# A two-expert combine on one core: the weights fetched as 16 long rows and turned by TensorE, in place of 128 short rows

## The chip, the cores and the metric

The kernel runs on one core of one Trainium2 chip. The metric is device time in microseconds (us), the median over several runs. Inside the core the work is done by TensorE (PE), VectorE (DVE), ScalarE (ACT) and GpSimd (POOL); SyncE (SP) issues transfers. Transfers between device memory and the on-chip memory are carried by 16 DMA engines, which two queues feed here: one that SP issues to (q1 in the profile) and one that ACT issues to (q10).

## The reference

Each of 16 x 1024 = 16384 tokens has two vectors of 512 numbers, one from each of its two experts, and two weights. The result is the weighted sum of the two vectors, in float32:

```
expert_outputs   (16, 1024, 2, 512)   float32
combine_weights  (16, 1024, 2)        float32
out[b, s, :] = expert_outputs[b, s, 0, :] * combine_weights[b, s, 0]
             + expert_outputs[b, s, 1, :] * combine_weights[b, s, 1]
```

There are 67 MB to read, 33.5 MB to write, and 131 KB of weights.

## The kernel before

**Layout.** The 16384 tokens are spread over 128 partitions, 128 tokens to a partition. The first 115 x 128 tokens (LAST = 115) are dealt out as 115 consecutive tokens per partition, the remaining 13 x 128 as 13 per partition; `rows` (lines 41 to 45) makes the views of both parts. A token's slot on a partition is its two expert vectors, 4 KB. The large tile `et` (line 58) has 51 such slots, divided into four rooms of 13, 13, 12 and 13 slots (lines 29 to 31). The tile `wt` (line 60) holds the weights in the form in which they are used: partition p has the two weights of each of its 128 tokens.

**Loop.** The tokens are worked in ten groups of 12 or 13 slots (line 32). Group g lies in room g mod 4. For each group `combine` (line 79) multiplies the whole room by its weights with one VectorE instruction (line 98) and adds the two halves with another (line 99), in place; the result goes back to device memory with one store (line 121). Group 8 (lines 87 to 95) and group 9 (lines 83 to 86) share the multiplication with ScalarE. When a room's store has landed, the load of the group four further on may go into it (line 124). So the fifth load waits for the first store, and so on.

**Queues.** All loads are issued by SP, in the order of the groups. The first one is in two parts (lines 110 and 111): two slots, cut into pieces of 4 KB, and the other 11. Loads two to four (groups 1 to 3) follow at once, as their rooms are free. The stores of groups 0 to 6 are issued by ACT, those of groups 7 to 9 by SP (line 120). The schedule is manual: each engine runs its instructions in the order in which they stand in the code, and waits where the data that it reads, or the room that it writes, isn't free.

**The start.** Before the loop three small transfers go to ACT's queue. VectorE fills a tile `zt` of 16 partitions x 128 numbers with zeros (line 102); ACT writes it to 16 places of the output, which are overwritten later (line 105). Then ACT fetches the weights with two transfers (lines 106 and 107): 128 rows of 115 x 2 numbers (920 bytes), one to each partition, and 128 rows of 13 x 2 numbers (104 bytes). VectorE's first multiplication (line 98) needs the weights and group 0.

Of the kernel before, what the change touches and what calls it, by code (L numbers as in the profile page):

```python
# [1 line left out]

# [4 lines left out]


@with_exitstack
def kernel(  # L10
    ctx: ExitStack,
    tc: tile.TileContext,
    expert_outputs: bass.AP,
    combine_weights: bass.AP,
    out: bass.AP,
):

    nc = tc.nc
    b, s, k, h = expert_outputs.shape
    assert k == 2
    n = b * s
    P = nc.NUM_PARTITIONS
    per = n // P
    assert per * P == n

    SIZES = [13, 13, 12, 13]
    ROOMS = len(SIZES)  # L30
    ROOM0 = [sum(SIZES[:r]) for r in range(ROOMS)]
    TILES = [13, 13, 12, 13, 13, 13, 12, 13, 13, 13]
    FIRST = [2, 11, 13, 12, 13]
    STORES = [[0], [1], [2], [3], [4], [5], [6], [7], [8], [9]]
    MIXED = {8: 3}
    LAST = 115
    N = len(TILES)
    assert sum(TILES) == per
    starts = [sum(TILES[:g]) for g in range(N)]

    def rows(x):

        first = x[0 : P * LAST, :].rearrange("(p t) f -> p t f", p=P)
        second = x[P * LAST : n, :].rearrange("(p t) f -> p t f", p=P)
        return lambda t, c: first[:, t : t + c, :] if t < LAST else second[:, t - LAST : t - LAST + c, :]

    flat = out.rearrange("b s h -> (b s) h")
    eo = rows(expert_outputs.rearrange("b s k h -> (b s) (k h)"))
    cw = rows(combine_weights.rearrange("b s k -> (b s) k"))
    o = rows(flat)  # L50

    dt = mybir.dt.float32
    mult = mybir.AluOpType.mult
    add = mybir.AluOpType.add
    copy = mybir.ActivationFunctionType.Copy

    pool = ctx.enter_context(tc.tile_pool(name="all", bufs=1))
    et = pool.tile([P, sum(SIZES), k * h], dt)
    halves = et.rearrange("p j (k h) -> p (j k) h", k=k)
    wt = pool.tile([P, per * k], dt)  # L60
    wk = wt.rearrange("p (t k) -> p t k", k=k)
    zt = pool.tile([16, 128], dt)
    warm = pool.tile([P, 1], dt)

    def load(g, skip=0, c=None, **kw):
        c = TILES[g] - skip if c is None else c
        at = ROOM0[g % ROOMS] + skip
        nc.sync.dma_start(out=et[:, at : at + c], in_=eo(starts[g] + skip, c), **kw)  # L68

    def weights(q, t, c):  # L70
        q.dma_start(out=wk[:, t : t + c, :], in_=cw(t, c))

    def pair(t, x0, x1, y):
        nc.scalar.activation(out=x0, in_=x0, func=copy, scale=wt[:, k * t : k * t + 1])  # L74
        nc.vector.scalar_tensor_tensor(  # L75
            out=y, in0=x1, scalar=wt[:, k * t + 1 : k * t + 2], in1=x0, op0=mult, op1=add
        )

    def combine(g, base):
        at, c, t0 = ROOM0[g % ROOMS], TILES[g], starts[g]  # L80
        room = halves[:, k * at : k * (at + c), :]
        x0, x1 = et[:, at : at + c, 0:h], et[:, at : at + c, h : 2 * h]
        if g == N - 1:
            for i in range(c):
                pair(t0 + i, x0[:, i, :], x1[:, i, :], halves[:, base + i, :])
            return
        if g in MIXED:
            v = MIXED[g]
            for i in range(v, c):
                x = x0[:, i, :]  # L90
                nc.scalar.activation(out=x, in_=x, func=copy, scale=wt[:, k * (t0 + i) : k * (t0 + i) + 1])  # L91
            w0 = wk[:, t0 : t0 + v, 0:1].to_broadcast([P, v, h])
            nc.vector.tensor_tensor(out=x0[:, 0:v, :], in0=x0[:, 0:v, :], in1=w0, op=mult)  # L93
            w1 = wk[:, t0 : t0 + c, 1:2].to_broadcast([P, c, h])
            nc.vector.tensor_tensor(out=x1, in0=x1, in1=w1, op=mult)  # L95
        else:
            wb = wt[:, k * t0 : k * (t0 + c)].unsqueeze(2).to_broadcast([P, k * c, h])
            nc.vector.tensor_tensor(out=room, in0=room, in1=wb, op=mult)  # L98
        nc.vector.tensor_tensor(out=halves[:, base : base + c, :], in0=x0, in1=x1, op=add)  # L99

    with tc.manual_schedule():
        nc.vector.memset(zt, 0.0)  # L102

        ahead = flat[0 : P * LAST, :].rearrange("(q t) h -> q (t h)", q=16)
        nc.scalar.dma_start(out=ahead[:, 0:128], in_=zt)  # L105
        weights(nc.scalar, 0, LAST)
        weights(nc.scalar, LAST, per - LAST)
        nc.scalar.activation(out=warm, in_=nc.const_aps.tensor(1.0, (P, 1), dt), func=copy)  # L108

        load(0, 0, 2, max_dma_last_dim=k * h * 4)  # L110
        load(0, 2)
        for g in range(1, ROOMS):
            load(g)
        for j, st in enumerate(STORES):
            base = k * ROOM0[st[0] % ROOMS if st != [N - 1] else (N - 4) % ROOMS]
            c = 0
            for g in st:
                combine(g, base + c)
                c += TILES[g]
            q = nc.sync if j >= 7 else nc.scalar  # L120
            q.dma_start(out=o(starts[st[0]], c), in_=halves[:, base : base + c, :])
            for g in st:
                if g + ROOMS < N:
                    load(g + ROOMS)


# [1 line left out]
_INS = ['expert_outputs', 'combine_weights']  # L128
_OUTS = [((16, 1024, 512), 'float32')]


# [23 lines left out]
```

## Time and profile before

| | |
|---|---|
| median of 3 runs | 239.11 us (239.08 to 239.14) |
| the profiled execution | 238.84 us |
| its span, first to last instruction | 237.1 us |
| VectorE busy | 190.0 us |
| ScalarE busy | 15.8 us |
| read / written in device memory | 67.24 MB / 33.56 MB |

The span is what the profile shows in detail; some 1.7 us of the execution's time lie around it. "Busy" counts the time in which an engine runs an instruction, not the time in which it waits. A packet is one piece of a transfer that one DMA engine moves: here, as a rule, what goes to one partition in one row, and 16 closing packets of 4 bytes with each transfer. A share in a row of a DMA queue is the packets' time, as a part of 16 engines over the stretch that was asked for; in short stretches a packet counts where it starts, so a share can be over 100%.

### The profile page before, as it was taken

How to read it: one execution, taken by the hardware profiler on the slowest of the kernel's cores; microseconds unless marked ns; L12 is line 12 of the kernel's file. 1: busy time of each engine (PE TensorE's matmuls, PEld its weight loads, DVE VectorE, ACT ScalarE, POOL GpSimd, SP SyncE). 2: the span in 40 equal slices, each digit the busy share in tenths (PEclk: the TensorE clock that was granted, in tenths of full speed). 3: DMA queues.
4: the chain of work that ended last, by engine and by line, in shares of the span. 5: the costliest groups of instructions: out<-in, count | busy, mean ns of one | idle time of the engine just before them, and what ended most of it. 6: DMA issues, size and time to landing. Idle time of an engine off the chain costs nothing.

```text
span 237.1 us, 154 instructions
## 1 busy us (share of the span) xinstructions
DVE 190.0 (80%) x33; ACT 15.8 (7%) x25; POOL 0.2 (0%) x4
## 2 busy tenths in 40 slices
DVE  0007999999999999999999997998499969919400
ACT  2000000000000000000000000000000055019200
POOL 0000000000000000000000000000000000000000
DMA  7999999999999999999899999999899999999996
GB/s 300 473 395 434 432 421 423 445 402 449 440 422 467 431 431 390 487 420 420 377 474 409 409 509 393 431 503 431 359 431 503 420 397 474 390 431 431 431 431 288
DMA packets 3472, 100.80 MB, mean 425 GB/s; under 512 B 512, under 2 KB 656, under 8 KB 912
## 3 DMA queue, kind: packets, MB, share of 16 engines
q1 hardware_dynamic: 2144, 77.33, 75.9%
q10 hardware_dynamic: 1328, 23.47, 23.0%
HBM read 67.24 MB, written 33.56 MB: 425 GB/s over the span
## 4 chain that ended last, share of the span: by engine, by line
DVE 53%; DMA 36%; issue 3%; ACT 0%; DVEq 0%; ACTq 0%; SPq 0%
DVE et L98 35%; DMA out_dram<-et 17%; DVE et L99 15%; DMA et<-in_expert_outputs_dram 12%; DMA wt<-in_combine_weights_dram 8%; DVE et L75 3%; ACT et L74 0%; DVEq L150 0%; ACTq L105 0%; DVE zt L102 0%; DVEq L98 0%; SPq L68 0%; ACTq L74 0%
## 5 line engine op out<-in xcount | busy, mean ns | idle before, releaser
L98 DVE TENSOR_TENSOR et<-et,wt 128x13312 f32<-128x13312 f32 (+1 forms) x8 | 110.0, 13754 | 23.7 <-DMA wt<-in_combine_weights_dram 18.5
L99 DVE TENSOR_TENSOR et<-et 128x6656 f32<-128x6656 f32 (+1 forms) x9 | 62.8, 6973 | 0.4
L91 ACT ACTIVATE et<-et,wt 128x512 f32<-128x512 f32 x10 | 6.2, 709 | 188.5 <-DMA et<-in_expert_outputs_dram 188.5
L75 DVE SCALAR_TENSOR_TENSOR et<-et,wt 128x512 f32<-128x512 f32 x13 | 8.7, 744 | 5.1 <-ACT et L74 5.1
L74 ACT ACTIVATE et<-et,wt 128x512 f32<-128x512 f32 x13 | 8.1, 712 | 14.0 <-DMA et<-in_expert_outputs_dram 14.0
L95 DVE TENSOR_TENSOR et<-et,wt 128x6656 f32<-128x6656 f32 x1 | 7.1, 7084 | 0.0
L93 DVE TENSOR_TENSOR et<-et,wt 128x1536 f32<-128x1536 f32 x1 | 1.8, 1759 | 2.2 <-DMA et<-in_expert_outputs_dram 2.2
L108 ACT ACT_TABLE_LOAD x1 | 1.3, 1283 | 2.4 <-issue 2.4
L102 DVE MEMSET zt<- 16x128 f32 x1 | 0.2, 165 | 0.8 <-PEq L139 0.8
L108 ACT ACTIVATE warm<-const-float32-1.0 128x1 f32<-128x1 f32 x1 | 0.2, 204 | 0.0
L139 POOL MEMSET const-bfloat16-1.0<- 128x1 bf16 x1 | 0.1, 102 | 0.0
L139 POOL MEMSET const-uint8-127<- 128x1 uint8 x1 | 0.1, 102 | 0.0
L139 POOL MEMSET const-float32-1.0<- 128x1 f32 x1 | 0.1, 99 | 0.0
L139 POOL MEMSET const-float32-0.0<- 128x1 f32 x1 | 0.1, 98 | 0.2 <-issue 0.2
## 6 DMA issues: line engine op xcount, KB each, us to landing
et<-in_expert_outputs_dram SPq DMA_DIRECT2D x7, 6656.0 KB, 32.2
out_dram<-et ACTq DMA_DIRECT2D x5, 3328.0 KB, 34.8
et<-in_expert_outputs_dram SPq DMA_DIRECT2D x2, 6144.0 KB, 41.0
out_dram<-et SPq DMA_DIRECT2D x3, 3328.0 KB, 20.0
out_dram<-et ACTq DMA_DIRECT2D x2, 3072.0 KB, 37.3
et<-in_expert_outputs_dram SPq DMA_DIRECT2D x1, 5632.0 KB, 18.0
et<-in_expert_outputs_dram SPq DMA_DIRECT2D x1, 1024.0 KB, 4.8
wt<-in_combine_weights_dram ACTq DMA_DIRECT2D x1, 115.0 KB, 18.0
```

What stands on the lines that cost most here:

```text
L74: nc.scalar.activation(out=x0, in_=x0, func=copy, scale=wt[:, k * t : k * t + 1])
L75: nc.vector.scalar_tensor_tensor(out=y, in0=x1, scalar=wt[:, k * t + 1 : k * t + 2], in1=x0, op0=mult, op1=add)
L91: nc.scalar.activation(out=x, in_=x, func=copy, scale=wt[:, k * (t0 + i) : k * (t0 + i) + 1])
L93: nc.vector.tensor_tensor(out=x0[:, 0:v, :], in0=x0[:, 0:v, :], in1=w0, op=mult)
L95: nc.vector.tensor_tensor(out=x1, in0=x1, in1=w1, op=mult)
L98: nc.vector.tensor_tensor(out=room, in0=room, in1=wb, op=mult)
L99: nc.vector.tensor_tensor(out=halves[:, base : base + c, :], in0=x0, in1=x1, op=add)
L102: nc.vector.memset(zt, 0.0)
L108: nc.scalar.activation(out=warm, in_=nc.const_aps.tensor(1.0, (P, 1), dt), func=copy)
L139: nc = _bacc.Bacc("TRN2", target_bir_lowering=False, num_devices=1)
```

## The change

- The zero tile, its memset and the write of it to the output are gone.
- The weights are fetched, still by two transfers on ACT's queue, as 16 rows each: the weights of the first 115 x 128 tokens are 16 contiguous rows of 1840 numbers (7360 bytes), those of the rest 16 rows of 208 (832 bytes). Row q goes to partition q and holds the weights of partitions 8q to 8q + 7 one behind the other.
- These rows (`sq`), an identity matrix (`ident`, filled by GpSimd) and an intermediate (`sb`) lie in the fourth room of `et`, which is not used yet.
- `spread` brings the weights to the partitions. They are cut into three parts (115, 115 and 26 columns of `wt`). For each part eight TensorE transposes of 16 partitions each write to PSUM, VectorE copies the result to `sb` while it reorders the columns from (r, q) to (q, r), and one more transpose turns the part back into a common PSUM tile `back`. At the end VectorE copies `back` to `wt`. Together 27 transposes and four copies.
- The load of group 3, which goes into the fourth room, stands behind `spread` and waits until the rows and the identity there are no longer read. Loads one to three go out as before.

```diff
-    zt = pool.tile([16, 128], dt)
+    Q = 16
+    M = k * LAST // 2
+    spare = et[:, ROOM0[3] : ROOM0[3] + 13, :].rearrange("p j f -> p (j f)")
+    sq, sb = spare[0:Q, 0 : per * k * P // Q], spare[:, 2048 : 2048 + 3 * P].rearrange("p (u x) -> p u x", u=3)
+    ident = spare[:, 4096 : 4096 + P]
+    psum = ctx.enter_context(tc.tile_pool(name="turn", bufs=1, space=bass.MemoryType.PSUM))
+    up = [psum.tile([P, P], dt, name=f"up{u}") for u in range(3)]
+    back = psum.tile([P, 2 * M + k * (per - LAST)], dt)
...
-    def weights(q, t, c):
-        q.dma_start(out=wk[:, t : t + c, :], in_=cw(t, c))
+    flatw = combine_weights.rearrange("b s k -> (b s k)")
+    PARTS = [(0, M), (M, M), (2 * M, k * (per - LAST))]
+    SPLIT = k * P * LAST
+
+    def weights():
+        nc.scalar.dma_start(out=sq[:, 0 : SPLIT // Q], in_=flatw[0:SPLIT].rearrange("(q x) -> q x", q=Q))
+        nc.scalar.dma_start(out=sq[:, SPLIT // Q :], in_=flatw[SPLIT:].rearrange("(q x) -> q x", q=Q))
+
+    def spread():
+        R = P // Q
+        for u, (a, c) in enumerate(PARTS):
+            row, off = (k * LAST, a) if u < 2 else (c, SPLIT // Q)
+            for r in range(R):
+                x = off + r * row
+                nc.tensor.transpose(up[u][0:c, r * Q : (r + 1) * Q], sq[:, x : x + c], ident[0:Q, 0:Q])
+            nc.vector.tensor_copy(
+                out=sb[0:c, u, :].rearrange("p (q r) -> p r q", r=R), in_=up[u][0:c, :].rearrange("p (r q) -> p r q", r=R)
+            )
+            nc.tensor.transpose(back[:, a : a + c], sb[0:c, u, :], ident[0:c, 0:c])
+        nc.vector.tensor_copy(out=wt, in_=back)
...
-        nc.vector.memset(zt, 0.0)
-
-        ahead = flat[0 : P * LAST, :].rearrange("(q t) h -> q (t h)", q=16)
-        nc.scalar.dma_start(out=ahead[:, 0:128], in_=zt)
-        weights(nc.scalar, 0, LAST)
-        weights(nc.scalar, LAST, per - LAST)
+        weights()
+        make_identity(nc, ident)
...
-        for g in range(1, ROOMS):
+        for g in range(1, ROOMS - 1):
             load(g)
+        spread()
+        load(ROOMS - 1)
```

1 line of the change is left out of this document (added).

## The prediction

> **What bounds the kernel now.** I read the page from the top (shares of the span, slices, queues), then the stretches of the span with their DMA share, then the waits, then single transfers with their time from issue to landing. First the page:
>
> ```profile
> span 237.1 us, 154 instructions
> ...
> DVE 190.0 (80%) x33; ACT 15.8 (7%) x25; POOL 0.2 (0%) x4
> ...
> DMA  7999999999999999999899999999899999999996
> ...
> DMA packets 3472, 100.80 MB, mean 425 GB/s; under 512 B 512, under 2 KB 656, under 8 KB 912
> ## 3 DMA queue, kind: packets, MB, share of 16 engines
> q1 hardware_dynamic: 2144, 77.33, 75.9%
> q10 hardware_dynamic: 1328, 23.47, 23.0%
> ```
>
> The two DMA queues (q1 is SP's, q10 ACT's) together keep the 16 DMA engines busy for 75.9 + 23.0 = 98.9% of the span, while VectorE, the busiest compute engine, stands at 80%. The reader is to see that the dips are in the first and the last slice only. The stretches say how long these ends are:
>
> ```profile
> 0.00:1.80 1.80, 0.17 (x1) 0.00 (x0) 0.20 (x4) 1.00 0.00 0
> 1.80:4.73 2.93, 0.00 (x0) 1.49 (x2) 0.00 (x0) 1.00 0.98 345
> ...
> 145.00:212.30 67.30, 56.49 (x7) 6.25 (x10) 0.00 (x0) 1.00 1.00 434
> ...
> 235.90:237.10 1.20, 0.00 (x0) 0.00 (x0) 0.00 (x0) 1.00 0.00 0
> ```
>
> Columns: stretch, its length, busy time of VectorE, ScalarE and GpSimd, granted clock, DMA share, GB/s. Nothing moves before 1.80 us and nothing after 235.90; between them the engines are full. So the time is 1.8 us of start, plus the work that the transfers put on each of 16 engines (about 234.1 us), plus 1.2 us of ending. A change moves the time if it alters that work, delays the first byte, or lets the engines run dry.
>
> The waits seem to say something else: VectorE's longest one is for the weights, 18.5 us at the very start.
>
> ```profile
> DVE et L98 <- DMA wt<-in_combine_weights_dram: 18.5, 1, 18.5
> DVE et L98 <- DMA et<-in_expert_outputs_dram: 5.2, 2, 4.0
> DVE et L75 <- ACT et L74: 5.1, 1, 5.1
> DVE et L93 <- DMA et<-in_expert_outputs_dram: 2.2, 1, 2.2
> 1.44 0.93 ACTq L71 DMA_DIRECT2D wt<-in_combine_weights_dram  x2
> 1.21 0.93 SPq L68 DMA_DIRECT2D et<-in_expert_outputs_dram  x2
> et<-in_expert_outputs_dram SPq DMA_DIRECT2D x1, 5632.0 KB, 18.0
> wt<-in_combine_weights_dram ACTq DMA_DIRECT2D x1, 115.0 KB, 18.0
> ```
>
> But the large weight transfer was issued at 1.44 and landed 18.0 us later, at 19.4; the 11 slots of the first load (5632 KB) were issued at 1.21 and also took 18.0, so they landed at 19.2. VectorE needs both. Behind the wait for the weights stands a wait for data that ends 0.2 us sooner.
>
> **The change part by part.**
>
> *Taken away: the zero write and the old weight transfers.* Their work on the DMA engines can be read, because for the first 35 us ACT's queue holds nothing else. ACT's row (and once SP's beside it) in the stretches 0 to 6, 6 to 19 and 19.5 to 35 us:
>
> ```profile
> q10 hardware_dynamic: 32, 0.01, 0.6%
> q1 hardware_dynamic: 144, 5.90, 104.8%
> q10 hardware_dynamic: 144, 0.12, 2.7%
> q10 hardware_dynamic: 144, 0.01, 0.7%
> ```
>
> Zero write: 0.6% of 6 us = 0.04 us. The 128 rows of 920 bytes, with 16 closing packets: 2.7% of 13 us = 0.35 us. The 128 rows of 104 bytes: 0.7% of 15.5 us = 0.11 us. Together 0.50 us, all on the path, as every engine is full. The middle pair also explains the lateness: 144 packets of one queue against 144 of the other, turn about, so each small row waits for one large load row. That was lateness, not work.
>
> *Put in their place: 16 rows of 7360 bytes and 16 of 832.* This is 131 KB, or 8192 bytes for each engine if each takes one row of each transfer. An engine moves 5.90 MB / 16 in 104.8% of 13 us (the q1 row above), 27.1 bytes per ns; the 104-byte rows say that a packet costs some 12 ns whatever it holds (0.109 us for 9 of them on each engine). So the low end of the price is 8192 / 27.1 = 0.30, with four packets' fixed part 0.32 us. The high end: the rows of before went to 128 partitions, these go to 16, and no row of this trace writes so few. If the limit is the way into a partition, and not the engine, 16 partitions take in one eighth of 434 GB/s (the stretch from 145 us), 54 GB/s, and 131 KB need 2.42 us. While they are in flight the engines that carry them do nothing else, so the price stands in full. The row nearest in shape is the zero write, 16 partitions at the ordinary 0.04 us, but it reads them and is 8 KB in all, too little to crowd anything. It speaks for the low half and decides nothing. I take the middle of the two ends as a ratio, the root of 0.32 x 2.42 = 0.88 us. Against the 0.50 us taken away that is +0.38 us; the ends are -0.18 and +1.92 us.
>
> [...]
>
> *VectorE's first start.* With the weights early it waits for the load alone, till 19.2 in place of 19.4. A gain of 0.2 us on an engine with 12.5 us of idle time behind it (5.2 + 5.1 + 2.2, the waits above) and off the bound: nothing. What is late next is the load, which ends when the engines have moved it.
>
> *The spread.* 27 transposes and four copies out of PSUM now stand ahead of VectorE's first multiply; GpSimd fills the identity meanwhile. No row shows TensorE, so I bound an instruction with its handover by the shortest and the longest small instruction of the trace:
>
> ```profile
> L139 POOL MEMSET const-uint8-127<- 128x1 uint8 x1 | 0.1, 102 | 0.0
> L75 DVE SCALAR_TENSOR_TENSOR et<-et,wt 128x512 f32<-128x512 f32 x13 | 8.7, 744 | 5.1 <-ACT et L74 5.1
> ```
>
> 31 x 0.10 = 3 us to 31 x 0.74 = 23 us. The weights should be in by 5 to 7 us: the zero write, first on that queue, landed 3.9 us after its issue (row below), and a row may have to let one large load row pass (45 KB / 27.1 = 1.7 us). So the spread ends between 8 and 30 us; its operands are mostly 16 wide, near the memset, so I take about 12. That is below 19.2, and costs nothing. At 30 us VectorE would start 10.8 us late; the 12.5 us of idle time absorb that, and the engines meanwhile have loads to move, as the next rows show. Without that cover up to 10.8 us would be lost.
>
> *The fourth load waits for the spread.* Its room holds the raw weights and the identity. It was issued at 5.54 and landed 71.0 us later, behind loads two and three:
>
> ```profile
> out_dram<-zt ACTq DMA_DIRECT2D x1, 8.0 KB, 3.9
> 1.72 0.94 SPq L68 DMA_DIRECT2D et<-in_expert_outputs_dram  x2
> 5.54 0.33 SPq L68 DMA_DIRECT2D et<-in_expert_outputs_dram  x1
> 67.72 0.33 SPq L68 DMA_DIRECT2D et<-in_expert_outputs_dram  x1
> et<-in_expert_outputs_dram SPq DMA_DIRECT2D x1, 6656.0 KB, 71.0
> et<-in_expert_outputs_dram SPq DMA_DIRECT2D x1, 6144.0 KB, 50.8
> 1.01 0.40 ACTq L105 DMA_DIRECT2D out_dram<-zt  x1
> 190.26 32.25 SPq L121 DMA_DIRECT2D out_dram<-et  x3
> out_dram<-et SPq DMA_DIRECT2D x1, 3328.0 KB, 14.1
> ```
>
> Load three (6144 KB, the second of the pair issued from 1.72 on, at about 2.2) lands after 50.8 us and holds SP's queue until 53. Issued at 12, or at 30, the fourth is in the queue long before its turn; behind it on SP stands load five, which before did not issue until 67.7 us. Cost nothing; past about 50 us it would let the queue run dry.
>
> *The end.* The last store is issued at 190.26 + 32.25, less its own issue, = 222.2 and lands after 14.1 us, yet 3328 KB need only 3328 x 1024 / 16 / 27.1 = 7.9 us: it queues about 5 us behind the store before it. So VectorE's end has some 5 us to spare, and shifts of its chain don't reach the time.
>
> *ACT's queue* loses the wait for the memset: its first transfer may go some 0.3 us sooner than at 1.01, beside SP's first load. Nothing gained, as the load starts the engines anyway; whether it pushes that load back is a case below.
>
> **Sum.** -0.50 + 0.88 = +0.38 us. The profiled execution took 238.84 us (span 237.1 and 1.7 around it), 0.27 us below the median of the runs, 239.11. I put the difference on the median: 239.49 us, 0.16% more. About 0.2%, 0.48 us, is what a measurement of this kernel can tell from no change: 238.63 to 239.59.
>
> **The rivals.**
>
> [...]
>
> *No crowd (no change).* The engine is the limit and the zero write's rate holds: 0.32 - 0.50 = -0.18 us, 238.93. For it: the zero write. Against: 8 KB can't show a crowd.
>
> *The weights ride in the start for nothing (faster).* In 2.93 us at 345 GB/s, (434 - 345) / 434 x 2.93 = 0.60 us of engine time goes unused. If the weights fit there, the whole 0.50 us is won: 238.61, just beyond the bound. Against: the stretch's share is already 0.98, so the packets do hold the engines.
>
> *The first load is pushed back, or the spread is later than its bound (slower).* Two issues at once, ACT's and SP's; ACT's issue of a weight transfer takes half of 0.93 us, so the first byte could move by 0.47 us: with the sum, 239.96.
>
> **How the numbers follow.** Forecast, a crowd paid in part, 239.2 to 239.7: 0.42. Paid in full, 239.82 and beyond: 0.31. None: 0.17. For nothing: 0.05. Pushed back: 0.05. Three quarters of the forecast's band lies inside 239.59: same 0.315 + 0.17 = 0.49; slower 0.105 + 0.31 + 0.05 = 0.46; faster 0.05. The range goes from just below the case without a crowd, 238.85, to 240.1, beyond the pushed-back case; the high end of the price, 241.03, stays out with the case that gains.
>
> **What would show it.** Weights landed by 7 us. The 18.5 us wait of line 98 put down to the load of the expert outputs, hardly shorter. Transposes ended by about 12 us, the fourth load issued right behind. Packets 3472 - 16 - 256 - 16 (one transfer's closing packets) + 32 = 3216. The last byte near 236.3 us. The crowd itself: ACT's queue share in the first 8 us, 0.32 us of work (4%) without it, about 0.9 us (11%) or more with it. The prediction is wrong if the engines show a gap after 5 us, if the first byte moves from 1.80, or if the price lies outside 0.3 to 1.5 us.

## The result, and the profile after

The changed kernel takes 239.45 us (median of 14 runs, 239.33 to 239.6), the kernel before, run beside it, 238.91 us (238.84 to 239.14): a ratio of 1.0021, 95% interval 1.0014 to 1.0028, that is 0.33 to 0.67 us slower. The forecast was 239.49 us, +0.38 us on the median then known. The value came out right, but not by its working. Below it is seen that one term of its sum was about 0.5 us too small and that a gain of about 0.4 us was not in it at all; and the kernel before came out 0.20 us lower than the 239.11 us on which the forecast was set, so that the change costs 0.54 us where 0.38 were forecast.

The profiled execution took 239.48 us. The page of the changed kernel, lines that answer to those shown of before:

```profile
span 237.7 us, 220 instructions
...
PE 4.9 (2%) x27; PEld 4.1 (2%) x27; DVE 191.4 (81%) x36; ACT 15.8 (7%) x25; POOL 0.7 (0%) x6
...
DMA  7999999989999999999899999999899999899996
...
DMA packets 3216, 100.80 MB, mean 424 GB/s; under 512 B 368, under 2 KB 384, under 8 KB 656
## 3 DMA queue, kind: packets, MB, share of 16 engines
q1 hardware_dynamic: 2144, 77.33, 75.8%
q10 hardware_dynamic: 1072, 23.46, 23.0%
```

The queues stand where they stood, at 98.8% of a span that is 0.6 us longer, and the packets are the 3216 that were counted ahead. ACT's queue has 256 packets less and the same share; a tenth of a per cent is 0.24 us there, so what the fewer packets saved, if anything, can't be seen in it.

The turning and VectorE's first start, from the changed kernel's timeline (start, us, engine and line, what, and in brackets the idle time before it with what ended it):

```profile
4.89 1.69 PE L94 MATMUL up<-et 16*115 16x16 f32 x8 [4.89 <-DMA et<-in_combine_weights_dram]
...
11.43 0.42 DVE L99 COPY wt<-back 128x256 f32<-128x256 f32 x1 [0.39 <-PE back L98]
20.32 14.03 DVE L126 TENSOR_TENSOR et<-et,wt 128x13312 f32<-128x13312 f32 x1 [8.46 <-DMA et<-in_expert_outputs_dram]
...
11.46 0.33 SPq L76 DMA_DIRECT2D et<-in_expert_outputs_dram  x1
```

The weights are in place at 11.9 us, as estimated, and the fourth load goes out at 11.46. VectorE then stands 8.5 us more, for the load alone, and starts at 20.32, where it started at 19.50 before. The weights come earlier and the data later.

How much later is read from the time from issue to landing of the first transfers. First the kernel before, then the changed one; the issues lie within 0.02 us of each other.

```profile
et<-in_expert_outputs_dram SPq DMA_DIRECT2D x1, 6656.0 KB, 33.3
et<-in_expert_outputs_dram SPq DMA_DIRECT2D x1, 6144.0 KB, 50.8
et<-in_expert_outputs_dram SPq DMA_DIRECT2D x1, 5632.0 KB, 18.0
et<-in_expert_outputs_dram SPq DMA_DIRECT2D x1, 1024.0 KB, 4.8
```

```profile
et<-in_expert_outputs_dram SPq DMA_DIRECT2D x1, 6656.0 KB, 34.2
et<-in_expert_outputs_dram SPq DMA_DIRECT2D x1, 6144.0 KB, 51.3
et<-in_expert_outputs_dram SPq DMA_DIRECT2D x1, 5632.0 KB, 19.0
et<-in_expert_outputs_dram SPq DMA_DIRECT2D x1, 1024.0 KB, 6.0
et<-in_combine_weights_dram ACTq DMA_DIRECT2D x1, 115.0 KB, 4.0
```

The first two slots (1024 KB) land 1.2 us later, the rest of group 0 (5632 KB) 1.0, load two (6656 KB) 0.9, load three (6144 KB) only 0.5 us later. So about 1.0 us is lost at the start and 0.4 us of it comes back between the landings of loads two and three. SP's queue from 42 to 46 us shows where, before and after:

```profile
q1 hardware_dynamic: 16, 0.79, 56.9%
```

```profile
q1 hardware_dynamic: 32, 1.57, 91.1%
```

Before, the 16 rows of 49152 bytes that start in these 4 us, as many as there are engines, take 0.569 x 4 = 2.28 us each on average. After, 32 such rows take 0.911 x 4 / 2 = 1.82 us each, which is the pace of the full stretches (49152 / 27.1 bytes per ns = 1.81). So in the kernel before each engine loses some 0.45 us here, just after the first store was issued (40.68 us), and in the changed kernel it doesn't. This is the "slow stretch between 40 and 50 us" of the expectations below.

From 46 us on little moves. The last load in the chain that ended last (start, us, what), before and after:

```profile
183.82 28.79 DMA et<-in_expert_outputs_dram
```

```profile
184.25 28.83 DMA et<-in_expert_outputs_dram
```

It lands at 213.08 against 212.61, 0.47 us later, and the span is 0.6 us longer.

Where the crowd sits is seen in the first 6 us, by queue. Before, and after:

```profile
q1 hardware_dynamic: 288, 1.77, 77.5%
q10 hardware_dynamic: 32, 0.01, 0.6%
```

```profile
q1 hardware_dynamic: 260, 1.25, 70.3%
q10 hardware_dynamic: 32, 0.12, 6.4%
```

The weights' own packets take 6.4% of 6 us = 0.38 us, little more than the low end of the price. But the load beside them moved 1.25 MB in 70.3% where it moved 1.77 MB in 77.5%: 3.4 us of packet time for a MB against 2.6. The price stands on the bill of the loads.

### The profile page after: what moved, and what is told of

The parts are those of the page before. It is cut to its first block, busy times and chain, and to the rows that moved or that the text cites. A ratio compares the mean times of both kernels' runs of the same rounds, so it can differ in the third digit from the quotient of the medians.

```text
span 237.7 us, 220 instructions
## 1 busy us (share of the span) xinstructions
PE 4.9 (2%) x27; PEld 4.1 (2%) x27; DVE 191.4 (81%) x36; ACT 15.8 (7%) x25; POOL 0.7 (0%) x6
## 2 busy tenths in 40 slices
DMA packets 3216, 100.80 MB, mean 424 GB/s; under 512 B 368, under 2 KB 384, under 8 KB 656
## 4 chain that ended last, share of the span: by engine, by line
DVE 50%; DMA 37%; issue 5%; another core or an unknown queue 1%; DVEq 0%; ACT 0%; SPq 0%; ACTq 0%
DVE et L126 35%; DMA et<-in_expert_outputs_dram 20%; DMA out_dram<-et 16%; DVE et L127 12%; DVE et L103 3%; ACT et L102 0%; DVEq L176 0%; SPq L76 0%; DVEq L126 0%; ACTq L102 0%
## 5 line engine op out<-in xcount | busy, mean ns | idle before, releaser
L95 DVE COPY et<-up 115x128 f32<-115x128 f32 (+1 forms) x3 | 1.1, 382 | 9.9 <-PE up L94 9.9
L94 PE MATMUL up<-et 16*115 16x16 f32 (+1 forms) x24 | 3.8, 295 | 5.0 <-DMA et<-in_combine_weights_dram 4.9
L94 PEld LDWEIGHTS up<-et 16*115 16x115 f32 (+1 forms) x24 | 3.5, 237 | 5.5 <-issue 5.1
L98 PE MATMUL back<-et 115*128 115x115 f32 (+1 forms) x3 | 1.2, 401 | 1.4 <-DVE et L95 1.4
L98 PEld LDWEIGHTS back<-et 115*128 115x128 f32 (+1 forms) x3 | 0.5, 180 | 1.8 <-DVE et L95 1.8
```

The lines of the kernel that those rows point to most:

```text
L94: nc.tensor.transpose(up[u][0:c, r * Q : (r + 1) * Q], sq[:, x : x + c], ident[0:Q, 0:Q])
L95: nc.vector.tensor_copy(out=sb[0:c, u, :].rearrange("p (q r) -> p r q", r=R), in_=up[u][0:c, :].rearrange("p (r q) -> p r q", r=R))
L98: nc.tensor.transpose(back[:, a : a + c], sb[0:c, u, :], ident[0:c, 0:c])
```

## The experiments

Two theories were set against each other. **Crowd**: 16 rows on 16 neighbouring partitions crowd the ways into them. **Start**: whatever runs beside the small pieces of the first load slows them. Further rivals were the turning, and the missing zero write. The kernel before ran beside each group of runs, with medians of 238.96, 238.92 and 238.91 us; in the first two groups one of its own runs (of 35, and of 18) took 241.1 us, and no profile was taken of such a run.

### The zero write taken away alone

```diff
-        nc.vector.memset(zt, 0.0)
-        ahead = flat[0 : P * LAST, :].rearrange("(q t) h -> q (t h)", q=16)
-        nc.scalar.dma_start(out=ahead[:, 0:128], in_=zt)
```

> The kernel before without its zero write and its memset; the weights still come as 128 short rows to 128 partitions, but are issued some 0.3 us sooner, beside the first load's 4 KB pieces. Theory crowd (16 rows on 16 neighbouring partitions crowd the way into them): nothing crowds here, the time is that of before, 238.9 us, less at most 0.04; the 4 KB pieces of the first load keep their mean of some 0.18 us. Rival start (whatever runs beside the first load's 4 KB pieces slows them, whatever its shape): slower by about 0.5 us, 239.4. Rival zero (the zero write itself was worth something): slower by some tenths too, but with the 4 KB pieces as before.

Measured: 239.75 us, ratio 1.0027 (1.0008 to 1.0046), but with runs from 238.91 to 240.9. The profiled one took 238.91 us, with the first loads landing nearly as before (5632 KB after 18.1 us, 1024 KB after 5.2 in place of 4.8). So 128 short rows early, beside the small pieces, cost nothing in that execution, which speaks against start. By its letter the slower median fits rival zero; whether the missing zero write is what the changed kernel loses is asked again with the zero write put back, below. What scatters the runs isn't known.

### The same 16 rows, on partitions that lie apart

```diff
+    wide = spare[0 : 7 * Q : 7, 6144 : 6144 + per * k * P // Q]
-        nc.scalar.dma_start(out=sq[:, 0 : SPLIT // Q], in_=flatw[0:SPLIT].rearrange("(q x) -> q x", q=Q))
-        nc.scalar.dma_start(out=sq[:, SPLIT // Q :], in_=flatw[SPLIT:].rearrange("(q x) -> q x", q=Q))
+        nc.scalar.dma_start(out=wide[:, 0 : SPLIT // Q], in_=flatw[0:SPLIT].rearrange("(q x) -> q x", q=Q))
+        nc.scalar.dma_start(out=wide[:, SPLIT // Q :], in_=flatw[SPLIT:].rearrange("(q x) -> q x", q=Q))
...
+        nc.gpsimd.memset(sq, 0.5)
```

> The changed kernel with its two weight transfers written to every seventh partition (0, 7, ... 105) in place of partitions 0 to 15; TensorE turns rows that GpSimd has filled with 0.5, so the weights used are not the real ones. Everything else, 16 rows of the same length at the same moment among it, is as in the changed kernel. Theory crowd: most of the price goes, the first load's small pieces go back to near 0.18 us each (0.234 in the changed kernel) and the time falls from 239.45 to between 238.8 and 239.0. Rival start: nothing changes, 239.4 to 239.5. Rival turning (TensorE, VectorE and the later fourth load are the price): 239.4 to 239.5 as well.

Measured: 238.94 us, ratio 1.0001 (0.9993 to 1.0010). The whole loss is gone. Three things besides the partitions differ from the changed kernel: the rows lie in another stretch of the room, the turning needn't wait for them, and they move later, though they were issued at the same moment. ACT's row in the changed kernel from 0 to 4 us, and here from 4 to 6 us (before 4 us ACT's queue moves nothing here; the trace has the first row at 4.47 us, in the changed kernel at 2.18):

```profile
q10 hardware_dynamic: 32, 0.12, 9.6%
```

```profile
q10 hardware_dynamic: 32, 0.12, 14.7%
```

The first 6 us and landings of this kernel:

```profile
q1 hardware_dynamic: 288, 1.77, 79.9%
q10 hardware_dynamic: 32, 0.12, 4.9%
...
et<-in_expert_outputs_dram SPq DMA_DIRECT2D x1, 6656.0 KB, 33.4
et<-in_expert_outputs_dram SPq DMA_DIRECT2D x1, 6144.0 KB, 50.9
et<-in_expert_outputs_dram SPq DMA_DIRECT2D x1, 5632.0 KB, 18.2
```

The load moves its 1.77 MB again, and lands nearly as before. Turning falls, as all of its work is still in this kernel. Start doesn't fall by this run alone, since the rows come when most of the small pieces are through; that the partitions count, and neither the moment nor the stretch of the room, is shown by three runs below: the zero write put back (still later rows, on partitions 0 to 15, and the loss is there), the transfer made twice (the second copy lies in the stretch used here and costs 1.09 us), and the added rows (crowded and apart at the same moment).

### The weights issued later

```diff
+        nc.scalar.activation(out=warm, in_=nc.const_aps.tensor(1.0, (P, 1), dt), func=copy)
         weights()
         make_identity(nc, ident)
-        nc.scalar.activation(out=warm, in_=nc.const_aps.tensor(1.0, (P, 1), dt), func=copy)
```

> The changed kernel with ScalarE's table load and warm-up put ahead of the weight transfers, which are issued some 1.5 us later (near 2.3 us) and so meet fewer of the 4 KB pieces. Theory crowd: the price stays, as the ways into the 16 partitions carry the same bytes whenever they come; 239.4 to 239.6, only the slowed packets are others, later ones. Rival start: the price falls by half or more, 238.9 to 239.2.

Measured: 239.44 us, ratio 1.0022 (1.0013 to 1.0030). It says nothing on the question, as the edit left the transfer where it was:

```profile
0.73 1.28 ACT L130 ACT_TABLE_LOAD   x1 [0.73 <-PEq L165]
0.79 0.40 ACTq L84 DMA_DIRECT2D et<-in_combine_weights_dram  x1
```

The transfer was issued at 0.79, while the table load ahead of it was still running. The question is answered by the zero write put back, below.

### The turning added to the kernel before

```diff
+        make_identity(nc, ident)
+        nc.gpsimd.memset(sq, 0.5)
...
-        for g in range(1, ROOMS):
+        for g in range(1, ROOMS - 1):
             load(g)
+        spread()
+        load(ROOMS - 1)
```

The last copy of `spread` goes to a tile of its own here.

> The kernel before, zero write and 128-row weights included, with the turning added: identity, 27 transposes of rows that GpSimd has filled, four copies by VectorE into a tile that nothing reads, and the fourth load behind them. Theory crowd: the turning costs nothing but the end of the program (one or two semaphores more), 238.9 to 239.05. Rival turning: 239.3 or more.

Measured: 238.94 us, ratio 0.9998 (0.9990 to 1.0007). The turning and the late fourth load cost nothing.

### The 16 rows added to the kernel before, in the middle of the loads

```diff
         weights(nc.scalar, LAST, per - LAST)
+        nc.scalar.dma_start(out=spare[0:16, 0 : k * P * LAST // 16], in_=flatw[0 : k * P * LAST].rearrange("(q x) -> q x", q=16))
```

> The kernel before with one more transfer at the end of its weight transfers: the 16 rows of 7360 bytes of the changed kernel, to partitions 0 to 15 of the fourth room, where nothing uses them; the fourth load waits for it. It runs near 36 us, in the middle of the large loads, far from the start. Theory crowd: an engine pays its own 0.28 us and three more of its neighbours', 1.1 us in all, 240.0 to 240.1. Rival start: only the bytes count there, +0.3 us, 239.25.

Measured: 239.49 us, ratio 1.0023 (1.0013 to 1.0033): 0.57 us, twice what start allows and half of what crowd does. The trace shows both the price and what made it look small. SP's and ACT's queue from 35.5 to 42 us, and SP's from 42 to 46:

```profile
q1 hardware_dynamic: 48, 2.36, 99.0%
q10 hardware_dynamic: 32, 0.12, 6.1%
...
q1 hardware_dynamic: 32, 1.57, 90.8%
```

At 27.1 bytes per ns the 2.36 MB of the loads need 5.44 us of each engine; they took 0.990 x 6.5 = 6.44, so the loads pay 1.0 us, and the added rows themselves took 0.061 x 6.5 = 0.40: 1.4 us in all, rather more than the 1.1 of crowd. From 42 to 46 us the rows then take 1.82 us each, as in the changed kernel, and not 2.28: the slow stretch is gone, which is worth some 0.45 us. That leaves about 0.95; this execution, the longest of the ten, took 239.76 us, 0.84 more than the kernel before.

### The same added rows, apart

```diff
-        nc.scalar.dma_start(out=spare[0:16, 0 : k * P * LAST // 16], in_=flatw[0 : k * P * LAST].rearrange("(q x) -> q x", q=16))
+        nc.scalar.dma_start(out=spare[0:112:7, 0 : k * P * LAST // 16], in_=flatw[0 : k * P * LAST].rearrange("(q x) -> q x", q=16))
```

> The same added transfer, written to every seventh partition (0, 7, ... 105). Theory crowd: its own 0.28 us and at most one neighbour's, 239.25 to 239.5, at least 0.5 us less than with partitions 0 to 15. Rival start: the same time as with partitions 0 to 15.

Measured: 239.92 us, with runs from 239.12 to 240.43, where the crowded one kept to 239.31 to 239.76; the ratio, 1.0027 (1.0001 to 1.0052), can't be told from the other. The expectation for the time was missed. The transfer itself is quicker apart (landed 37.0 us after its issue, crowded 37.6), and the same stretches, in the profiled execution of 239.66 us, show why the time isn't:

```profile
q1 hardware_dynamic: 48, 2.36, 91.3%
q10 hardware_dynamic: 32, 0.12, 4.7%
...
q1 hardware_dynamic: 32, 1.57, 105.6%
```

For the same 2.36 MB the loads need 0.913 x 6.5 = 5.93 us here, 0.5 more than 5.44, and the added rows took 0.31: 0.8 us in all in place of 1.4, at the same moment and for the same bytes. That is the 0.5 us or more that crowd expected. But from 42 to 46 us the rows of the loads take 2.11 us each in place of 1.82, so the two on each engine lose the 0.6 us again: the slow stretch is still there and hides the gain. Why the runs scatter so widely stays open.

### The large 16-row transfer made twice

```diff
+        again = spare[0:Q, 6144 : 6144 + SPLIT // Q]
+        nc.scalar.dma_start(out=again, in_=flatw[0:SPLIT].rearrange("(q x) -> q x", q=Q))
```

> The changed kernel with its large 16-row transfer made twice, the second copy to another stretch of the same 16 partitions. Theory crowd: a second price of about 1.1 us, 240.5. Rival start (small pieces slowed by whatever runs beside them): +0.3 to +0.5 us, 239.75 to 239.95. What was given back later in the changed kernel (0.6 us between 40 and 50 us) is given back only once.

Measured: 240.54 us (four runs, 240.50 to 240.57), ratio 1.0067 (1.0051 to 1.0083). A second price of 1.09 us on the time:

```profile
et<-in_expert_outputs_dram SPq DMA_DIRECT2D x1, 6656.0 KB, 35.5
et<-in_expert_outputs_dram SPq DMA_DIRECT2D x1, 6144.0 KB, 52.5
et<-in_expert_outputs_dram SPq DMA_DIRECT2D x1, 5632.0 KB, 20.3
```

The 11 slots land 1.3 us later than with one transfer. One engine by itself would need an estimated 7360 bytes / 27.1 bytes per ns = 0.27 us for its row; the price on the time is four times that, the one on the landing nearly five times. What came back between loads two and three comes back once (their times from issue to landing differ by 52.5 - 35.5 = 17.0 us, in the changed kernel by 17.1, before by 17.5).

### The loads shifted, without a crowd

```diff
-        nc.scalar.dma_start(out=ahead[:, 0:128], in_=zt)
+        nc.sync.dma_start(out=ahead[:, 0:128], in_=zt)
```

> The kernel before with its zero write issued by SP, ahead of the loads, in place of ACT: every load starts some 0.6 to 0.8 us later, and nothing crowds. It asks why the changed kernel has no slow stretch between 40 and 50 us. If that stretch is tied to the moment in the run, or goes away with any delay of the loads, it is gone here too and the time is near that of before, 238.9 to 239.2. If it went because of the crowd, it is still here, and the time is 239.5 to 239.75.

Measured: 240.96 us (four runs, 240.26 to 241.48), ratio 1.0083 (1.0059 to 1.0107), longer than either case of the expectation. The loads go out 0.7 us later, at 1.44, and 2 us are lost. SP's queue from 42 to 46 us:

```profile
q1 hardware_dynamic: 26, 1.28, 93.3%
```

The rows take 2.30 us each there (0.933 x 4 x 16 / 26), as before: the slow stretch is still here, and a mere delay of the loads doesn't bring the 0.4 us back. What makes the loss so large isn't explained.

### 32 rows on 32 partitions

```diff
-    Q = 16
+    Q = 32
```

> The changed kernel with 32 rows of half the length (3680 and 416 bytes) on partitions 0 to 31 in place of 16 on 0 to 15; the rest follows (four transposes to a part). Theory crowd: the rows land on twice as many ways in, so an engine pays for one neighbour in place of three: 0.3 us of own work and 0.3 us of crowd, 239.45 - 0.6 = 238.85 if the slow stretch between 40 and 50 us stays away, 239.3 to 239.45 if it comes back with the smaller crowd. Rival start: as the changed kernel, 239.4 to 239.5.

Measured: 239.10 us (238.95 to 241.14), ratio 1.0023 (1.0002 to 1.0043). Nine of the eleven runs lie between 238.95 and 239.2, with a median of 239.04, 0.13 us above the kernel before; the other two lie at 241.1 us, where single runs of the kernel before were seen too. By the ratio the loss is unclear, by the nine it is a quarter of that of the changed kernel, and neither 238.85 nor 239.3 to 239.45 was met.

```profile
et<-in_expert_outputs_dram SPq DMA_DIRECT2D x1, 6656.0 KB, 33.7
et<-in_expert_outputs_dram SPq DMA_DIRECT2D x1, 6144.0 KB, 50.9
et<-in_expert_outputs_dram SPq DMA_DIRECT2D x1, 5632.0 KB, 18.5
```

The first load is delayed by half (0.5 in place of 1.0 us), as crowd says, and loads two and three are 17.2 us apart: 0.3 of the 0.4 us comes back here too, which is why the time shows less than half of the loss.

### A small crowd

```diff
-        nc.scalar.dma_start(out=spare[0:16, 0 : k * P * LAST // 16], in_=flatw[0 : k * P * LAST].rearrange("(q x) -> q x", q=16))
+        nc.scalar.dma_start(out=spare[0:16, 0:208], in_=flatw[0:3328].rearrange("(q x) -> q x", q=16))
```

> The kernel before with an added transfer of 16 rows of 832 bytes to partitions 0 to 15 (the added 7360-byte rows, made nine times shorter), near 36 us. Theory crowd for its price: 0.04 us of own work and 0.1 us of crowd. On the slow stretch between 40 and 50 us: if the crowd takes it away by putting the engines in another order, a small one may do, and the time is 238.4 to 238.6; if it takes it away in proportion (data read ahead while the writes are held up covers a later stall of the reads), 0.1 us of crowd saves 0.1 us and the time is that of before, 238.9 to 239.05.

Measured: 238.96 us, ratio 1.0003 (0.9994 to 1.0012). Nothing is won: 16 rows of 832 bytes didn't bring the return here, and the rows of the loads from 42 to 46 us take 2.1 us each.

### The zero write put back into the changed kernel

```diff
+        nc.vector.memset(zt, 0.0)
+        ahead = flat[0 : P * LAST, :].rearrange("(q t) h -> q (t h)", q=16)
+        nc.scalar.dma_start(out=ahead[:, 0:128], in_=zt)
         weights()
```

> The changed kernel with the zero write put back ahead of the 16-row transfers. Theory crowd: the zero write is 0.04 us of work, 239.45 to 239.5. Rival zero (the loss comes from taking the zero write away): back to 238.9 to 239.0.

Measured: 239.56 us, ratio 1.0025 (1.0015 to 1.0035). The loss isn't that of the zero write. And as the zero write holds the weights back, this is also the run that "late" was meant to be. ACT's queue from 6 to 9 us, where the large 16-row transfer now runs, and the landings:

```profile
q10 hardware_dynamic: 16, 0.12, 11.5%
...
et<-in_expert_outputs_dram SPq DMA_DIRECT2D x1, 6656.0 KB, 34.7
et<-in_expert_outputs_dram SPq DMA_DIRECT2D x1, 6144.0 KB, 51.7
et<-in_expert_outputs_dram SPq DMA_DIRECT2D x1, 5632.0 KB, 19.5
et<-in_expert_outputs_dram SPq DMA_DIRECT2D x1, 1024.0 KB, 5.1
et<-in_combine_weights_dram ACTq DMA_DIRECT2D x1, 115.0 KB, 9.0
```

The weights land 9.0 us after their issue in place of 4.0. The small pieces, landed at 5.8 us, are through by then and back near their old time (5.1 against 4.8 us), and the 11 slots behind them pay instead, 19.5. So start falls: the price doesn't hang on the small pieces; here the 11 slots that run beside the rows pay it. (The profile is of the longest of the nine runs, 239.80 us, so its 19.5 is rather high.)

### A second profile without the zero write

> The kernel before without its zero write once more, for a second profile: its runs lay between 238.91 and 240.9 and the first profile was of the fastest. If the scatter comes from the stretch between 40 and 50 us, this profile has a longer slow stretch there and nothing else that is new; if from the start, its first loads land late.

One execution, 238.89 us, again at the lower end (5632 KB after 18.2 us), so it can't answer the question. Where the longer ones lose their time stays open.

## Why the prediction was right, point by point

- **What bounds the kernel**: right that the DMA engines bound it (98.8% of the span after the change); wrong that they are full from 1.80 to 235.90 us. The view that the prediction reads has a stretch with a share of 0.97 and 409 GB/s, which it didn't show:

```profile
35.00:62.00 27.00, 26.97 (x4) 0.00 (x0) 0.00 (x0) 1.00 0.97 409
```

In it lie the 4 us in which the kernel before loses 0.45 us and the changed one doesn't.
- **The wait for the weights hides a wait for the load**: right. It became a wait for the load, and ended later, not 0.2 us sooner, as the load was late.
- **The turning, the identity, the fourth load**: right, 0 us, and 11.9 us against the estimate of about 12. Only the small weight transfer was late: issued at 1.20, it landed 9.0 us later, at 10.2 and not by 7, and the last part of the turning waited 0.4 us for it.
- **Taken away, 0.50 us**: not contradicted; it can't be seen by itself, since taking away the zero write alone scattered the runs.
- **The price of the 16 rows, 0.88 us**: too small, and the step that failed is the middle of the two ends. (The low end is also added wrongly: four packets at 12 ns make 0.35 us and not 0.32, and the middle 0.92; that changes nothing.) The 11 slots land 1.0 us later although 0.04 + 0.35 us of old work before them is gone: 1.4 us by the tenths of these rows, 1.3 for the second transfer in "twice". The case "paid in full", 239.82 us, meant 0.71 + 0.50 = 1.21 us and came nearest; the row of the zero write, taken as a hint towards the low half, misled. The factor of four in it (1.21 against the 0.30 us of one engine) was the author's supposition, and so are the neighbours, three or one, that an engine pays for in the expectations: no run shows how many rows hold each other up. What the runs show in its place is the price: 1.09 us on the time for the second transfer in "twice", four times the 0.27 us of one engine, and with 32 rows half the delay of the 11 slots, 0.5 in place of 1.0 us.
- **Not in the sum at all**: the 0.4 us that came back between loads two and three. Of 1.4 - 0.50 - 0.4 the rest is 0.5 us, and 0.54 was measured. So the value was near the mark by luck: an undersized price met an unforeseen return, and the median of the kernel before, 0.20 us higher when the forecast was made, made up for the rest. That the rows crowd on 16 neighbouring partitions was right (1.4 us there, and with the rows apart 238.94 us and no loss); the working was not.
- **The sign that would show it**: wrong place. ACT's queue was to show 11% of the first 8 us or more with a crowd. It was 5.3%, 0.42 us, which by that sign would have meant hardly any crowd:

```profile
q10 hardware_dynamic: 50, 0.13, 5.3%
```

The crowd shows in SP's queue (3.4 us of packet time for a MB against 2.6) and in landings (the 11 slots 1.0 us later). That the price would stand on the rows' own packets was a second error of this step.
- **Rivals**: no crowd (238.93 us), and weights for nothing in the start (238.61), fall with the time itself, and with "apart" and "twice". Paid in full is true of the price and not of the time. The first load pushed back: its first byte still comes at 1.80 us; its pieces were late through the crowd, and with the rows apart its 11 slots land after 18.2 us, against 18.0 before.

What brings 0.4 us back is not settled. It goes with the crowd and not with a delay. The rows that SP's queue starts from 42 to 46 us (share x 4 us x 16 / packets, as above) take 1.82 us on average in all five kernels with 16 full rows on 16 neighbouring partitions (the changed one, "late", "twice", "zero_back" and the added rows), 1.87 with half a crowd, and 2.1 to 2.4 in all others: 2.28 before, 2.42 with the rows apart, 2.30 with the loads shifted, 2.1 with the small crowd. The times of loads two and three say the same (17.0 or 17.1 us apart in "twice", "zero_back" and the changed kernel, 17.2 with half a crowd, 17.5 before and with the rows apart). What holds the rows up there, and why a crowd ahead of it takes that away, no run shows.

## What to carry to other kernels

A small transfer cost more than its bytes here, where the DMA engines are full: 131 KB on 16 neighbouring partitions cost some 1.4 us, against the 0.30 us that 8192 bytes need on one engine at 27.1 bytes per ns, and the same rows on partitions seven apart no more than the short rows that they replaced (238.94 against 238.96 us). Added in the middle of the loads, rows apart cost 0.8 us where crowded ones cost 1.4, but the time didn't show it, as another stretch lost it again: read such a price where it is paid, and then what the time makes of it. Look for it in the landing times of the large transfers beside it, not in the small one's own packets. And before a wait is taken away, see which wait ends next: here it was 0.2 us behind, so there was nothing to win.

## What the runs showed that was not expected

- The zero write is 0.04 us of work, and without it, with the short rows kept, runs of one and the same kernel lay between 238.91 and 240.9 us. The changed kernel has no zero write and keeps to 239.33 to 239.6, so its absence alone doesn't do it. Scatter of the same size came with the added rows apart (239.12 to 240.43) and with the zero write on SP's queue (240.26 to 241.48). The kernel before itself had two runs at 241.1 us and one at 239.4 among 53 in the first two groups, and the 32 rows had two of eleven at 241.1. The cause is open; both profiles without the zero write are of executions near 238.9 us.
- A transfer that stands behind an activation on ScalarE was issued at 0.79 us, while that activation's table load ran from 0.73 to 2.01: the order of the instructions did not delay it here.
- No version beat the kernel before. The rows apart equal it at 238.94 us, with rows of 0.5 turned in place of the weights.
